# Two half-height products of a filter step, issued one right behind the other

## The chip, the cores and the metric

The kernel runs on one core of a Trainium2 chip. The metric is device time in microseconds (us) of one execution; less is better. Engines are named as in the profile: PE is TensorE (matrix products), PEld its weight loads, DVE is VectorE, ACT is ScalarE, POOL is GpSimd, SP is SyncE, which here only issues DMAs. Each engine works through its own list of instructions in order and waits at an instruction until what it needs is there.

## The reference

The reference is one layer of a hybrid encoder over a sequence of 2048 positions with 1024 channels: an input projection, a Hyena group (long convolutions with generated filters), an mLSTM group, an output projection, cross-attention and an MLP. The change touches only the generation of the Hyena filters, a small network over position features, whose last layer has 64 inputs:

```python
def _hyena_filter_spectrum(L, w1, b1, fr1, w2, b2, fr2, w3):
    ...
    hid = jnp.sin(fr1.astype(f32) * (z @ w1.astype(f32) + b1.astype(f32)))
    hid = jnp.sin(fr2.astype(f32) * (hid @ w2.astype(f32) + b2.astype(f32)))
    filt = (hid @ w3.astype(f32)).reshape(L, HYENA_ORDER, FILTER_DIRS, D_HYENA)
    ...
    filt = filt * jnp.exp(-t * jnp.abs(deltas))[:, None, None, :]
    fwd = filt[:, :, 0]
    bwd = jnp.flip(filt[1:, :, 1], axis=0)
    two_sided = jnp.concatenate([fwd, jnp.zeros((1, HYENA_ORDER, D_HYENA), f32), bwd], axis=0)
    return jnp.fft.rfft(two_sided, axis=0)
```

There are two orders and two directions, so 4 x 512 filter channels. Forward and backward filters are windowed, joined and transformed; the transforms are matrix products with constant matrices.

## The kernel before

The program is a string of stages. Two generators are woven into each other: `filters` with the first part of the input projection (`sweep`), then `hyena` with the rest of it; the mLSTM, the attention and the MLP follow. Weaving gives the order in which the instructions are written down. The order in which they stand on each engine is drawn from that by a scheduler, which works with a timeline of its own, so a changed dependency can move instructions far behind it.

The projection's products are the background work of PE. A product in high precision is split into three products of F32R halves (`mm3`, L336 to L338), each 128 x 128 by 512 columns, accumulated in a bank `mm`. Its results are copied by ACT (L685), convolved over three positions by ACT and DVE (L699 to L702), turned by PE (L719, 128-column products in which the identity is an operand), copied by ACT or DVE (L174, L176) and stored. New weights are split by ACT and DVE (L341, in `split`), new columns of `x` are scaled by DVE (L461) and split.

`filters` first computes the hidden layer `hid` (L239, L243, with the sine in between on DVE and ACT). `hid` holds two copies of the 64 hidden units: partitions 0 to 63 for forward positions, 64 to 127 for backward ones. The output layer then runs in 32 steps (16 blocks of positions by 2 orders). Each step:

- takes two banks `hy`, `pf` and `pb`;
- L286 multiplies `hid[0:64]` with `w3[0:64]` into `pf`, L287 multiplies `hid[64:128]` with `w3[64:128]` into `pb`. Both are plain fp32 products over 64 partitions, half of the array's height, and each leaves two records in the trace;
- DVE multiplies both with the decay windows (L289 reads `pf`, L290 reads `pb`), which ends the use of the banks;
- DVE adds the two (L294), POOL subtracts them (L295);
- `front` of the step before is issued (`late` holds it back by one step): two full-height fp32 products with `f1` (L271) into two more banks `hy`, ACT copies them out (L272), and SP stores them as `fs` every second step (L274).

There are four banks `hy`, taken in turn. A step takes four: two for L286 and L287, two for the L271 of the step before it. So the banks of a step's L286 and L287 are those that L286 and L287 of the previous step had, and they come free when DVE has run that step's L289 and L290. L286 waits for the first of them, L287 for the second, each by itself, and the scheduler may put other products between the two.

After the 32 steps the second transform follows (`blocks`): SP loads `fs` back (L305) and matrices (L301), PE multiplies (L319), ACT copies (L320), SP stores `hd` (L321). `hyena` reads `hd` later; its forward products are L856 and L880, its inverse ones L846 and L899.

Of the kernel before, what the change touches and what calls it, by code (L numbers as in the profile page):

```python
# [9 lines left out]
F32 = mybir.dt.float32  # L10
# [115 lines left out]
class Prog:  # L126
    def __init__(self, ctx, tc, a):
        self.tc, self.nc, self.a = tc, tc.nc, a
        nc = self.nc
        self.ctx = ctx  # L130
        self.dr = ctx.enter_context(tc.tile_pool(name="dr", bufs=1, space=DRAM))
        self.s = {}
        cp = self.cp = ctx.enter_context(tc.tile_pool(name="cp", bufs=1))
        ident = cp.tile([128, 128], F32, name="ident")
        nc.gpsimd.memset(ident, 1.0)
        nc.gpsimd.affine_select(ident, ident, pattern=[[-1, 128]], compare_op=ALU.is_equal, fill=0.0,
                                base=0, channel_multiplier=1)
        self.ident = ident
        self.eps = cp.tile([128, 1], F32, name="eps")
        nc.vector.memset(self.eps, EPS)  # L140
        self.ones = cp.tile([128, 128], F32, name="ones")
        nc.vector.memset(self.ones, 1.0)
        self.flip = 0
        self.pending = []
        self.prepq = None
        self.mid = None
        self.rbp = cp.tile([128, 16], F32, name="rbp")
        par = self.par = cp.tile([128, 192], F32, name="par")
        nc.scalar.dma_start(out=par, in_=a["par"])
        self.g_mix, self.g_mem, self.gx, self.gf = (par[:, 8 * i:8 * i + 8] for i in range(4))  # L150
        self.cw = par[:, 32:92].rearrange("p (i c) -> p i c", i=3)
        self.cb, self.gb = par[:, 92:112], par[:, 112:128]
        self.ps = ctx.enter_context(tc.tile_pool(name="ps", bufs=1, space=PSUM))
# [2 lines left out]
        return self.ps.tile([128, 512], F32, tag="mm", name="mm", bufs=4)  # L156

    def hy(self):
        return self.ps.tile([128, 512], F32, tag="hy", name="hy", bufs=4)

    def dram(self, name, shape):
        if name not in self.s:
# [42 lines left out]
    def filters(self):  # L205
        nc, tc, a = self.nc, self.tc, self.a
# [3 lines left out]
        if True:  # L210
            fw = sb.tile([128, 1280], F32, name="fw")
            nc.scalar.dma_start(out=fw, in_=a["fw"])
            w1, w2, w3 = fw[0:66, 0:128], fw[:, 128:256], fw[:, 256:1280].rearrange("p (o c) -> p o c", o=2)
# [18 lines left out]
            hid = sb.tile([128, 16, 128], F32, name="hid")  # L232
# [17 lines left out]
            def windows(j2):  # L250
                if j2 == 8:
                    return None
                w = ta(), ta()
                for r in range(2):
                    d = nc.sync.dma_start(out=w[r], in_=wv[r, :, 2 * j2:2 * j2 + 2])
                    if j2 < 2:
                        tc.keep_in_program_order(d)
                return w

            held = []  # L260

            def late(f):
                if held:
                    held.pop()()
                if f is not None:
                    held.append(f)

            def front(e, st, jj, o, js):
                for p in range(2):
                    pp = self.hy()  # L270
                    nc.tensor.matmul(pp, f1[:, p], e[p], start=True, stop=True)  # L271
                    nc.scalar.copy(st[p][:, jj], pp)  # L272
                    if jj == 1:
                        nc.sync.dma_start(out=sd[o][p, :, js], in_=st[p])  # L274

            nxt = windows(0)
            for j2 in range(8):
                js = slice(2 * j2, 2 * j2 + 2)
                yield 14
                (wf, wb), nxt = nxt, windows(j2 + 1)  # L280
                for o in range(2):
                    st = [ta() for p in range(2)]
                    for jj in range(2):
                        j = 2 * j2 + jj
                        pf, pb = self.hy(), self.hy()
                        nc.tensor.matmul(pf, hid[0:64, j], w3[0:64, o], start=True, stop=True)  # L286
                        nc.tensor.matmul(pb, hid[64:128, j], w3[64:128, o], start=True, stop=True)  # L287
                        f, b = tb(), tb()
                        nc.vector.tensor_tensor(f, pf, wf[:, jj], ALU.mult)  # L289
                        nc.vector.tensor_tensor(b, pb, wb[:, jj], ALU.mult)  # L290
                        if j == 0:
                            nc.vector.tensor_tensor(f[0:1], f[0:1], (skip, skip2)[o][0:1], ALU.add)
                        e = [tb() for p in range(2)]
                        nc.vector.tensor_tensor(e[0], f, b, ALU.add)  # L294
                        nc.gpsimd.tensor_tensor(e[1], f, b, ALU.subtract)  # L295
                        late(lambda e=e, st=st, jj=jj, o=o, js=js: front(e, st, jj, o, js))
# [13 lines left out]
            for n, (o, i) in enumerate(order):  # L310
                if True:
                    yield 3.4
                    dm, t = q.pop(0)
# [14 lines left out]
    def ta(self):  # L328
        return self.fsb.tile([128, 2, CH], F32, tag="a", name="a", bufs=7)

    def tb(self):
        return self.fsb.tile([128, CH], F32, tag="b", name="b", bufs=8)
# [1535 lines left out]
```

## Time and profile before

| | |
|---|---|
| median of 3 runs | 3330.34 us (3326.27 to 3330.63) |
| profiled execution | 3330.7 us |
| its span, first to last instruction | 3329.0 us |
| mean granted clock of PE | 0.980 |
| DMA | 655.70 MB, mean 197 GB/s |
| records of L286 and of L287 | 64 each, from 119.6 to 348.5 us |
| records of L271 | 128, from 127.6 to 357.0 us |
| records of L319 | 128, from 364.7 to 483.7 us |

A profile shows one execution. In a row of the timeline stand start, duration, engine, line, operation, tiles (out<-in), shape and count, then in brackets the idle time of the engine before it. A matrix product's duration is from its start until its last result, and products overlap in the array, so what a product costs PE is read from the distance of starts. "Waits" are times in which an engine stood idle before an instruction, by what released it. In tables by stretches each row is one window of the span.

### The profile page before, as it was taken

The numbers are of one execution on the slowest core, as the hardware profiler recorded it, in microseconds if no ns is written. First come the engines' busy times: TensorE is split into PE (matmuls) and PEld (weight loads), VectorE is DVE, ScalarE is ACT, GpSimd is POOL, SyncE is SP. The second block draws the span as 40 slices with busy tenths as digits, with TensorE's granted clock in tenths as the row PEclk, the third lists the DMA queues.
The fourth block names the chain that finished last, engine by engine and source line by source line (L and its number), as shares of the span: only waits on it lengthen the run. The fifth ranks groups of instructions, "written<-read, shape, count | busy, mean of one in ns | idle before, by whom it ended". The sixth has DMA issues, their size and how long they took to land.

```text
span 3329.0 us, 45394 instructions
## 1 busy us (share of the span) xinstructions
PE 3162.2 (95%) x15293; PEld 2519.0 (76%) x15293; DVE 1985.2 (60%) x3334; ACT 1512.1 (45%) x2860; POOL 1253.5 (38%) x863
## 2 busy tenths in 40 slices
PE   6999999899999988699999998999999999999998
PEld 5655666667667887598888896888788887888876
DVE  7684324534556656576766564755755576656595
ACT  5442444642564344354454444555655543333335
POOL 0132000220122204634434114876765564434483
PEclk9999999999999999799999999999999999999999
DMA  5554897886787659857557525764754475444434
GB/s 177 177 195 135 284 316 244 241 262 237 217 225 251 211 182 310 262 155 246 172 179 238 191 89 175 229 216 155 222 172 144 161 240 169 127 143 138 130 93 167
DMA packets 472257, 655.70 MB, mean 197 GB/s; under 512 B 39630, under 2 KB 251854, under 8 KB 471000
## 3 DMA queue, kind: packets, MB, share of 16 engines
q1 hardware_dynamic: 436404, 594.23, 56.4%
q10 hardware_dynamic: 35620, 58.57, 4.8%
q8 instruction: 121, 1.98, 0.3%
q14 instruction: 112, 0.92, 0.1%
HBM read 437.67 MB, written 214.99 MB: 196 GB/s over the span
## 4 chain that ended last, share of the span: by engine, by line
PE 49%; DMA 4%; DVE 3%; issue 2%; POOL 1%; ACT 1%; SPq 0%; DVEq 0%; POOLq 0%; ACTq 0%
PE mm L338 10%; PE mm L336 10%; PE mm L337 10%; PE hy L338 5%; PE hy L336 5%; PE hy L337 5%; DMA rw<-rows 1%; DVE wl L341 1%; PE hy L1135 1%; DMA wr<-xs 1%; PE hy L1137 1%; PE hy L1370 0%; PE hy L1266 0%; DMA wn<-in_w_out_dram 0%; DMA wr<-in_ff_w_dram 0%
## 5 line engine op out<-in xcount | busy, mean ns | idle before, releaser
L341 DVE TENSOR_TENSOR wl<-wn,wh 128x512 fp32r<-128x512 f32 (+1 forms) x364 | 293.5, 841 | 124.3 <-ACT wh L341 111.4
L1449 DVE TENSOR_TENSOR bl<-wr,bh 128x512 fp32r<-128x512 f32 x213 | 239.0, 1128 | 130.5 <-ACT bh L1448 126.8
L1448 ACT CAST ah<-w 128x512 fp32r<-128x512 f32 x284 | 176.2, 622 | 301.0 <-PE hy L337 152.2
L885 POOL TENSOR_TENSOR b<-b,a 128x512 f32<-128x512 f32 x64 | 89.4, 1397 | 586.7 <-ACT b L883 351.1
L341 ACT CAST wh<-wn 128x512 fp32r<-128x512 f32 (+1 forms) x364 | 208.9, 618 | 198.3 <-PE mm L337 54.9
L336 PE MATMUL mm<-xh,wh 128*128 128x512 f32 x640 | 279.4, 438 | 6.6 <-ACT xh L496 2.7
L337 PE MATMUL mm<-xl,wh 128*128 128x512 f32 x640 | 276.8, 433 | 0.1
L338 PE MATMUL mm<-xh,wl 128*128 128x512 f32 x640 | 265.8, 416 | 0.0
L1449 DVE TENSOR_TENSOR al<-w,ah 128x512 fp32r<-128x512 f32 x236 | 219.1, 930 | 58.6 <-ACT ah L1448 58.3
L1448 ACT CAST bh<-wr 128x512 fp32r<-128x512 f32 x232 | 143.6, 621 | 235.7 <-PE mm L338 171.3
L338 PE MATMUL mm<-bh,al 128*128 128x512 f32 x576 | 225.5, 394 | 7.4 <-DVE al L1449 4.5
L336 PE MATMUL mm<-bh,ah 128*128 128x512 f32 x576 | 226.8, 394 | 0.1
L337 PE MATMUL mm<-bl,ah 128*128 128x512 f32 x576 | 225.8, 392 | 0.0
L336 PE MATMUL mm<-act,wh 128*128 128x512 f32 x512 | 200.1, 395 | 1.0 <-ACT wh L341 1.0
L337 PE MATMUL mm<-act,wh 128*128 128x512 f32 x512 | 200.7, 392 | 0.0
L338 PE MATMUL mm<-act,wl 128*128 128x512 f32 x512 | 199.1, 392 | 0.0
L1305 POOL TENSOR_TENSOR ssum<-ssum,sq 128x512 f32<-128x512 f32 x56 | 79.0, 1411 | 277.4 <-ACT sq L1304 274.3
L336 PE MATMUL hy<-bh,ah 128*128 128x512 f32 x448 | 175.2, 391 | 0.0
L337 PE MATMUL hy<-bl,ah 128*128 128x512 f32 x448 | 174.6, 390 | 0.0
L338 PE MATMUL hy<-bh,al 128*128 128x512 f32 x448 | 174.4, 390 | 0.0
L295 POOL TENSOR_TENSOR b<-b 128x512 f32<-128x512 f32 x32 | 66.5, 2079 | 284.6 <-DVE b L290 147.8
L336 PEld LDWEIGHTS mm<-xh,wh 128*128 128x128 f32 x640 | 122.2, 191 | 63.9 <-issue 29.1
(360 smaller groups left out, 8922.9 us busy)
## 6 DMA issues: line engine op xcount, KB each, us to landing
wr<-hc SPq DMA_DIRECT2D x224, 256.0 KB
w<-in_ff_w_dram SPq DMA_DIRECT2D x176, 256.0 KB
hc<-t SPq DMA_DIRECT2D x128, 256.0 KB
wn<-in_w_in_dram SPq DMA_DIRECT2D x100, 256.0 KB
hc<-q SPq DMA_DIRECT2D x96, 256.0 KB
fs<-a SPq DMA_DIRECT2D x32, 512.0 KB
a<-fs SPq DMA_DIRECT2D x32, 512.0 KB
hd<-a SPq DMA_DIRECT2D x32, 512.0 KB
```

The source lines that it names most:

```text
L295: nc.gpsimd.tensor_tensor(e[1], f, b, ALU.subtract)
L336: mm(ps, lh, rh, start=start, stop=False)
L337: mm(ps, lh, rl, start=False, stop=False)
L338: mm(ps, ll, rh, start=False, stop=stop)
L341: both = (self.nc.scalar.copy(hi, src), self.nc.vector.tensor_tensor(lo, src, hi.bitcast(F32), ALU.subtract))
L885: nc.gpsimd.tensor_tensor(xt, xt, hi[:, m], ALU.mult)
L1135: nc.tensor.matmul(dst, nm[:, h], va[:, h], start=True, stop=state is None)
L1137: nc.tensor.matmul(dst, rows_[d, 1][:, h], state[:, h], start=False, stop=True)
L1305: nc.gpsimd.tensor_tensor(ssum, ssum, sq, ALU.add)
L1448: self.nc.scalar.copy(hi, src)
L1449: eng.tensor_tensor(lo, src, hi.bitcast(F32), ALU.subtract)
```

## The change

L286 and L287 are now issued by a helper, `beside`. It writes down the second product (into `pb`) first. It looks up, in a new list of the names of all `hy` banks taken so far, the two tiles that held the places of `pf` and `pb` four tiles before, finds the last instruction that read each of them, and makes the second product wait for both. The first product (into `pf`) is written down behind it, with a high priority, and pinned behind the last product written before it on PE, that is behind the second product. The products, their operands, the banks and all other instructions are as they were, and each engine has as many instructions as before.

```diff
     def hy(self):
-        return self.ps.tile([128, 512], F32, tag="hy", name="hy", bufs=4)
+        t = self.ps.tile([128, 512], F32, tag="hy", name="hy", bufs=4)
+        self.banks.append(t[:, 0:1].tensor.name)
+        return t
+
+    def beside(self, first, second):
+        n = self.banks.index(first[0].tensor.name)
+        n = self.banks.index(first[0].tensor.name)
+        held = self.banks[max(0, n - 4):max(0, n - 2)]
+        b = self.nc.tensor.matmul(*second, start=True, stop=True)
+        for i in reversed(self.nc.cur_bb.bb.instructions[-4000:]):
+            own = [x.bass_ap.tensor.name for x in i.ins if getattr(x, "bass_ap", None) is not None]
+            for t in [t for t in held if t in own]:
+                held.remove(t)
+                self.tc.add_manual_dep(b.ins, i.name, mybir.DependencyInfo(
+                    mybir.DependencyClass.Sync, mybir.DependencyReason.DATA), reason="beside")
+        with self.tc.high_priority(2000):
+            self.tc.keep_in_program_order(self.nc.tensor.matmul(*first, start=True, stop=True))
...
                         pf, pb = self.hy(), self.hy()
-                        nc.tensor.matmul(pf, hid[0:64, j], w3[0:64, o], start=True, stop=True)
-                        nc.tensor.matmul(pb, hid[64:128, j], w3[64:128, o], start=True, stop=True)
+                        self.beside((pf, hid[0:64, j], w3[0:64, o]), (pb, hid[64:128, j], w3[64:128, o]))
                         f, b = tb(), tb()
```

In the changed file the second product stands at L168, the first at L176, and all lines behind them are 16 to 17 later.

More of the change, by code (lines that the diff above doesn't have):

```diff
@@ L143, in __init__ @@
         self.flip = 0
+        self.banks = []
         self.pending = []
```

## The prediction

> **What bounds the kernel now.** I read the page first, for the share of each engine.
>
> ```profile
> span 3329.0 us, 45394 instructions
> PE 3162.2 (95%) x15293; PEld 2519.0 (76%) x15293; DVE 1985.2 (60%) x3334; ACT 1512.1 (45%) x2860; POOL 1253.5 (38%) x863
> ```
>
> PE is busy for 95% of the span and no other engine passes 60%. That is an average, so the table by stretches comes next. The columns are: stretch, its length, then busy time and count on PE, PEld, DVE, ACT, POOL, then granted clock, DMA share, GB/s. The first row is the stage of the change, the second its most crowded part, then the filters' second transform, the Hyena convolutions, the mLSTM's start.
>
> ```profile
> 119.00:350.00 231.00, 231.00 (x795) 129.82 (x794) 142.63 (x228) 83.08 (x133) 64.32 (x31) 1.00 0.46 153
> 160.00:205.00 45.00, 45.00 (x165) 27.11 (x165) 38.96 (x82) 19.81 (x30) 16.84 (x6) 1.00 0.53 178
> 350.00:500.00 150.00, 148.94 (x584) 100.70 (x583) 36.06 (x54) 67.10 (x114) 2.22 (x1) 1.00 0.94 323
> 500.00:1166.00 666.00, 637.28 (x3056) 469.88 (x3055) 358.42 (x595) 324.98 (x525) 124.33 (x86) 0.99 0.75 236
> 1166.00:1500.00 334.00, 277.23 (x1830) 254.25 (x1830) 201.77 (x533) 140.91 (x369) 124.50 (x98) 0.92 0.74 228
> ```
>
> In the stage of the change PE is busy 231.00 of 231.00 us at full clock: nothing but PE's own work sets its length. The waits of the stage, over all engines, say the same from the other side.
>
> ```profile
> POOL b L295 <- DVE b L290: 141.2, 28, 8.7
> ACT a L272 <- PE hy L271: 95.5, 45, 6.2
> DVE b L289 <- PE hy L286: 47.1, 17, 4.9
> DVE b L290 <- PE hy L287: 16.7, 18, 2.0
> ```
>
> DVE stands still 47.1 us for L286 and 16.7 us for L287, and ACT 95.5 us for L271: the readers of the banks wait for the products, not the products for the readers.
>
> **The change part by part.** *Pairing.* First the number of steps that it reaches. The records of L286 (count, shortest, median and longest in ns, first and last start), then the same table for L286 alone, for L287 alone, and for every product of `hid`, that is for both together:
>
> ```profile
> L286 PE MATMUL hy<-fw,hid x64: 589/589/693, 119.6 to 346.4; 64*128 64x512 f32 x64
> ...
> 119.00:350.00 231.00, 35.65 (x64) 9.50 (x64) 1.00 0.46 153
> 119.00:350.00 231.00, 35.65 (x64) 9.50 (x64) 1.00 0.46 153
> 119.00:350.00 231.00, 61.52 (x128) 16.33 (x128) 0.00 (x0) 1.00 0.46 153
> ```
>
> Each product leaves two records, so 64 are 32 steps, at 35.65 / 32 = 1.11 us. Together they cover 61.52 us, not 71.30: 9.78 us lie on top of each other, 9.78 / 1.11 = 9 steps. Those 9 are the ones in which nothing stands between the two products; in the other 23 something does. In the built order of the changed program all 32 stand with nothing between. Here is one step of each kind on PE (start, duration, line, tile, count), the split one first.
>
> ```profile
> 252.12 0.39 PE L336 MATMUL mm<-xh,wh 128*128 128x512 f32 x1
> 252.34 0.39 PE L337 MATMUL mm<-xl,wh 128*128 128x512 f32 x1
> 252.66 1.12 PE L286 MATMUL hy<-fw,hid 64*128 64x512 f32 x2
> 253.71 0.50 PE L338 MATMUL mm<-xh,wl 128*128 128x512 f32 x1
> 254.14 1.12 PE L287 MATMUL hy<-fw,hid 64*128 64x512 f32 x2
> 255.20 1.12 PE L271 MATMUL hy<-b,f 128*128 128x512 f32 x2
> ...
> 289.30 0.39 PE L338 MATMUL mm<-xh,wl 128*128 128x512 f32 x1
> 289.53 0.39 PE L336 MATMUL mm<-xh,wh 128*128 128x512 f32 x1
> 289.85 0.69 PE L286 MATMUL hy<-fw,hid 64*128 64x512 f32 x1
> 289.85 0.69 PE L287 MATMUL hy<-fw,hid 64*128 64x512 f32 x1
> 290.38 0.59 PE L286 MATMUL hy<-fw,hid 64*128 64x512 f32 x1
> 290.39 0.59 PE L287 MATMUL hy<-fw,hid 64*128 64x512 f32 x1
> 290.91 0.50 PE L337 MATMUL mm<-xl,wh 128*128 128x512 f32 x1
> 291.24 0.39 PE L338 MATMUL mm<-xh,wl 128*128 128x512 f32 x1
> ```
>
> Read starts, since durations overlap. An ordinary product of the projection holds PE 0.23 us (289.30 to 289.53). The one before a half-height product takes 0.32 (252.34 to 252.66) and the one behind it 0.33 (290.91 to 291.24): going into and out of the half-height form costs 0.09 and 0.10. The split step, from 252.34 to 255.20, is 2.86 us; less two ordinary slots (0.46), plus the way out that the L271 behind it hides (0.10), it is 2.50 us. The paired step, from 289.53 to 291.24, is 1.71 less 0.46, so 1.25 us: both products run in the time of one. A step that becomes a pair frees 2.50 - 1.25 = 1.25 us, and 23 of them free 28.7 us, all on the engine that sets the stage's length. No instruction is added or removed on any engine, and the 32 steps keep their own DMAs.
>
> *The hold.* Now L287 goes first and waits until DVE has read both banks of the step before, by L289 and by L290; L286 follows. Before, L286 waited for L289 alone. Behind the waiting product stands the projection on PE, and for that wait ACT (L685 and the splits), then DVE and the stores. The readers' rows (mean ns after the busy time), then a typical and the tightest step on DVE, and the first and last split step of that part on PE:
>
> ```profile
> L289 DVE TENSOR_TENSOR b<-hy,a 128x512 f32<-128x512 f32 x32 | 22.0, 688 | 50.3 <-PE hy L286 47.1 <-issue 2.0 <-PE hy L287 1.1
> L290 DVE TENSOR_TENSOR b<-hy,a 128x512 f32<-128x512 f32 x32 | 21.9, 686 | 16.7 <-PE hy L287 16.7
> L295 POOL TENSOR_TENSOR b<-b 128x512 f32<-128x512 f32 x31 | 64.3, 2075 | 277.9 <-DVE b L290 141.2 <-DVE P L680 122.5 <-PE hy L271 7.9
> ```
>
> ```profile
> 247.63 0.69 DVE L290 TENSOR_TENSOR b<-hy,a 128x512 f32<-128x512 f32 x1 [0.60 <-PE hy L287]
> 253.89 0.69 DVE L289 TENSOR_TENSOR b<-hy,a 128x512 f32<-128x512 f32 x1 [4.24 <-PE hy L286]
> ...
> 188.10 0.68 DVE L290 TENSOR_TENSOR b<-hy,a 128x512 f32<-128x512 f32 x1
> ```
>
> ```profile
> 164.71 1.12 PE L286 MATMUL hy<-fw,hid 64*128 64x512 f32 x2
> ...
> 189.74 1.12 PE L286 MATMUL hy<-fw,hid 64*128 64x512 f32 x2
> ```
>
> Typically L290 ends at 248.32 and the next step's first product starts at 252.66: 4.3 us to spare. In the crowded part it ends at 188.78 against 189.74: 0.96 us to spare. There DVE does 38.96 us of work in 45, since the next columns of `x` are prepared then. Three of the steps between 160 and 205 are split, the first at 164.71, the last at 189.74; pairing brings PE 3 x 1.25 = 3.8 us forward there, 2.8 us beyond the spare. Bounds: no gain below nothing, as PE has no idle time to lose, and at most one L290 in each of 31 steps, 31 x 0.69 = 21.3 us. I take 3 us, by the tightest row. The other consumers have room: a step lasts (346.4 - 119.6) / 31 = 7.3 us by the first and last start of L286, of which POOL's L295 needs 2.08, and from the start of L286 to the end of L295 pass 1.23 (252.66 to 253.89) + 0.69 + 0.69 + 2.08, about 4.7 us, while the L271 that needs it stands behind the next pair.
>
> A rule that speaks against pairing stands in the Trainium skill, TensorEngine Tiling (Array Packing), section PSUM Bottleneck: products that run side by side speed up TensorE but not the reading of the banks, which may become the limit. Here the two reads take 0.69 + 0.69 = 1.38 us against 1.06 for the pair, so by that rule the pair would be paced by DVE; the trace disagrees on average, since those 1.38 us come once in 7.3, and comes near to it from 160 to 205 alone.
>
> *The order behind it.* The scheduler draws the order anew up to the middle of the program. The products of the second transform (L319) stand on average 39 places later against the projection, the Hyena's inverse products (L846) 19 later at first and not at all from their middle on; in the mLSTM some products change places. At 0.23 us, 39 places are 9 us of projection that used to lie behind the filters, as cover for the Hyena's chain, and now lies before it. What such cover is worth, the longest waits of PE from 350 to 1166 show:
>
> ```profile
> PE hy L846 <- DVE b L886: 7.4, 7, 1.6
> PE mm L336 <- ACT st L174: 6.2, 3, 4.0
> PE mm L743 <- DVE st L176: 5.0, 1, 5.0
> ```
>
> PE idles 666 - 637.28 = 28.7 us from 500 to 1166, in pieces of a microsecond to five. Bounds: 9 us lost if all of the cover is missed; 11 us won if the waits of 6.2 and 5.0 are dissolved by chance. I take 4 lost, since the chain already waits there. For the mLSTM (334 - 277.23 = 56.8 us idle) I take nothing, with 8 to either side by the size of a few such waits. From 350 to 500 DMA is at 0.94, but PE is busy 148.94 of 150: that stretch moves forward as a whole.
>
> *The sum.* The profiled execution took 3330.7 us (span 3329.0): 3330.7 - 28.7 + 3 + 4 = 3309.0. The median of the runs, 3330.34, is 0.4 below the profiled one, so 3308.6; I say 3309.
>
> **The rivals.**
> 1. *The Hyena gives most of it back.* The convolutions' chain, not PE, sets when the stage ends, and PE waits longer in it. For: 28.7 us of idle PE already, and 9 us less cover. Against: PE is busy 637.28 of 666. With 9 us of cover, 8 in the mLSTM and 3 for the hold gone, 28.7 - 20 = 9 are left: 3322.
> 2. *The pair does not overlap in the new order.* All 9 pairs in the trace have L286 ahead; now L287 is. Were they to run one after the other, 23 steps would save one way in and out (0.2 us each, 4.6) and 9 would lose 1.05 each (252.66 to 253.71; 9.5): 3335. Against: 0.01 us between the starts (290.38, 290.39) shows no preference for a side.
> 3. *Slower: the hold becomes a stall at the head of PE's queue.* L290 stands on DVE behind work of the projection (L341, L176) whose products lie behind the held L287; the two queues then take turns instead of overlapping. A turn costs the way from product to reader, 1.23, plus 0.69 for L290, 1.9 us. It decides from 28.7 / 31 = 0.93 us a step on; with 20 of 31 steps caught it is 38 us, so 3340. For: DVE is busy 142.63 of 202 us once the stage is shorter, 71%, and 38.96 of 41 in the crowd. Against: 4.3 us to spare in the typical step, and DVE's 63.8 us of waiting for just these products.
> 4. *DVE's reads set the pace* wherever it is crowded: none of the 3.8 us from 160 to 205 is kept. That is 1 us beyond my 3, and gives 3310; it lies inside the forecast.
>
> **How the numbers follow.** Forecast with rival 4: 65%, its own range 3296 (28.7 and half of the 11 won) to 3317 (hold 3, cover 9, and 3 of the mLSTM lost). Rival 1, from 3317 to 3327: 14%. Rival 2, 3327 to 3337: 7%. Rival 3: 9%. More than 34 us won: 5%. The range 3295 to 3327 leaves out some 2 in 10. About 0.2%, 6.7 us, is what a measurement here can tell from no change, so faster means below 3323.7: the forecast, the larger gain and two thirds of rival 1, 0.79. Slower means above 3337: rival 3 and the edge of 2, 0.10. The rest, 0.11, is the same.
>
> **What would show each step.** Pairing: all 32 steps with L286 and L287 starting within 0.01 us, and the products of `hid` covering about 36 us in place of 61.52. Its worth: the time from the first start of L286 to the last down from 227 us to between 198 and 204. The hold: waits of PE at L287's new line for DVE, 3 us in total and in the crowded part alone; above 29 us it is rival 3. The order: PE's idle time in the Hyena's 666 us at 28.7 before, about 33 after; if it is over 45, rival 1. I am wrong at the root if the stage shortens by less than 15 us although all pairs overlap, for then something other than PE held it.

## The result and the profile after

The changed kernel takes 3301.7 us (median of 4 runs, 3294.94 to 3305.1) against 3330.49 before: ratio 0.9911, 95% interval 0.9896 to 0.9925, so 25 to 35 us less. Measured again later (e11 below), the ratio was 0.9921, 0.9904 to 0.9937. The profiled execution took 3300.1 us. Its page begins:

```profile
span 3298.4 us, 45399 instructions
PE 3131.6 (95%) x15293; PEld 2510.5 (76%) x15293; DVE 1989.7 (60%) x3334; ACT 1513.6 (46%) x2860; POOL 1246.8 (38%) x863
```

PE has 30.6 us less to do and the span is 30.6 us shorter, with the same 15293 records. The row of the products of `hid`, from the table by stretches, and a step on PE (in the new file L168 is the product into `pb`, L176 the one into `pf`, L288 what was L271):

```profile
119.00:340.00 221.00, 36.45 (x128) 9.72 (x128) 0.00 (x0) 0.99 0.51 168
```

```profile
251.74 0.62 PE L735 MATMUL mm<-ident,cv 128*65 128x128 f32 x4
252.29 0.69 PE L168 MATMUL hy<-fw,hid 64*128 64x512 f32 x1
252.30 0.69 PE L176 MATMUL hy<-fw,hid 64*128 64x512 f32 x1
252.83 0.59 PE L168 MATMUL hy<-fw,hid 64*128 64x512 f32 x1
252.84 0.59 PE L176 MATMUL hy<-fw,hid 64*128 64x512 f32 x1
253.35 1.13 PE L288 MATMUL hy<-b,f 128*128 128x512 f32 x2
```

All 32 steps look like this one: the two products start within 0.01 us of each other, and together they cover 36.45 us in place of 61.52.

To see where the time came from, stretches of equal work have to be compared. The new order moves some projection products into the filters' stage, so equal names are not equal work; I divided both traces at the same counts of PE records instead (the x after PE's busy time). Columns as in the prediction. First before, then after: the filters' output layer, the first part of the Hyena, its second part, the start of the mLSTM, the rest.

```profile
119.00:360.00 241.00, 241.00 (x840) 136.98 (x839) 147.11 (x234) 87.08 (x140) 66.54 (x32) 1.00 0.48 159
...
465.00:674.00 209.00, 198.99 (x802) 138.77 (x801) 96.56 (x149) 111.67 (x173) 28.27 (x20) 0.98 0.78 246
674.00:1167.00 493.00, 474.05 (x2402) 356.60 (x2401) 272.15 (x462) 227.07 (x376) 96.06 (x66) 0.99 0.74 234
1167.00:1498.00 331.00, 274.23 (x1805) 251.25 (x1804) 199.55 (x528) 139.88 (x366) 124.50 (x98) 0.92 0.74 228
1498.00:3329.00 1831.00, 1779.95 (x8691) 1498.99 (x8689) 1162.95 (x1748) 830.18 (x1590) 937.39 (x641) 0.99 0.54 173
```

```profile
119.00:338.00 219.00, 214.18 (x843) 131.99 (x841) 148.45 (x235) 86.23 (x137) 61.68 (x32) 0.99 0.51 167
...
443.00:646.00 203.00, 199.17 (x802) 137.20 (x800) 95.39 (x144) 113.08 (x174) 25.72 (x19) 0.99 0.85 268
646.00:1142.00 496.00, 476.17 (x2402) 358.44 (x2401) 276.83 (x465) 230.16 (x381) 99.07 (x69) 0.98 0.75 234
1142.00:1470.00 328.00, 271.02 (x1806) 247.86 (x1805) 196.02 (x526) 140.21 (x366) 123.03 (x97) 0.92 0.74 228
1470.00:3298.00 1828.00, 1777.79 (x8693) 1497.78 (x8691) 1165.77 (x1750) 830.19 (x1590) 935.67 (x641) 0.99 0.54 173
```

The filters' stretch gives 22 us, the Hyena's first part 6; the second part loses 3, and the mLSTM and the rest give 3 each. In the filters' stretch PE's busy time fell by 26.8 us, but PE, which never idled there before, now idles 4.8 us (219.00 - 214.18). PE's waits in that stretch say why:

```profile
PE mm L352 <- ACT xh L357: 2.5, 1, 2.5
PE mm L469 <- DVE dg L463: 0.7, 1, 0.7
PE hy L288 <- DVE xr_y L219: 0.6, 1, 0.6
PE hy L168 <- DVE b L306: 0.4, 2, 0.2
PE mm L353 <- DVE xl L357: 0.4, 1, 0.4
PE hy L288 <- POOL b L311: 0.2, 1, 0.2
```

The held product L168 waited 0.4 us in all. Most of the rest is for the preparation of `x`, which comes late around 180 us. The longest wait, of 2.5 us, ends with the cast of `xh` on ACT. Here are that cast and the one before it on ACT, then the scaling on DVE whose result it reads:

```profile
180.30 0.62 ACT L357 CAST wh<-wn 128x512 fp32r<-128x512 f32 x1 [4.83 <-DMA wn<-in_w_in_dram]
180.83 1.04 ACT L357 CAST xh<-xt 128x1024 fp32r<-128x1024 f32 x1
...
177.41 1.40 DVE L477 SCALAR_TENSOR_TENSOR xt<-xt,par,rb 128x512 f32<-128x512 f32 x2
```

DVE was done with `xt` at 178.81, but the cast began only at 180.83: before it on ACT stands the cast of new weights, and for their transfer ACT had been idle for 4.83 us. So some 2.0 of these 2.5 us, an estimate from the three rows, come by way of a late transfer. SP issued it at 175.49, and had waited before that for DVE to free buffers (4.8, 3.2 and 0.8 us from 163 on); as far as these waits show, DVE's crowd of work stands at the start of this chain. After the longest wait the granted clock falls to half for a while (row of the stretch just behind it; the clock stands ahead of the DMA share):

```profile
183.20:186.20 3.00, 2.64 (x8) 1.48 (x5) 3.00 (x5) 1.06 (x2) 3.00 (x1) 0.51 1.01 361
```

The whole stretch has 0.99, so 1% of 219 us or some 2 us more went there. DVE waits for the products less than before, yet still does (rows of all engines' waits; before, 47.1 us for the first product and 16.7 for the second):

```profile
DVE b L305 <- PE hy L176: 33.6, 18, 4.3
ACT P L701 <- PE mm L354: 22.5, 13, 4.8
```

In the Hyena's first part PE's waits were, before and after:

```profile
PE mm L336 <- ACT st L174: 4.0, 1, 4.0
PE hy L846 <- DVE b L886: 2.6, 3, 1.3
PE hy L846 <- ACT cv L704: 2.4, 1, 2.4
```

```profile
PE hy L862 <- DVE b L902: 3.2, 3, 1.9
```

Two waits of 4.0 and 2.4 us have gone: the redrawn order won there, where the prediction had it lose.

### The profile page after: what moved, and what is told of

Same layout as the page of the kernel before. It is cut to its first block, busy times and chain, and to the rows that moved or that the text cites. A ratio compares the mean times of both kernels' runs of the same rounds, so it can differ in the third digit from the quotient of the medians.

```text
span 3298.4 us, 45399 instructions
## 1 busy us (share of the span) xinstructions
PE 3131.6 (95%) x15293; PEld 2510.5 (76%) x15293; DVE 1989.7 (60%) x3334; ACT 1513.6 (46%) x2860; POOL 1246.8 (38%) x863
## 4 chain that ended last, share of the span: by engine, by line
PE 75%; DMA 10%; DVE 5%; issue 4%; ACT 3%; POOL 2%; SPq 1%; ACTq 0%; DVEq 0%; POOLq 0%
PE mm L352 15%; PE mm L354 15%; PE mm L353 15%; PE hy L352 5%; PE hy L354 5%; PE hy L353 5%; DMA a<-hd 2%; PE hy L872 2%; PE hy L335 2%; PE hy L288 2%; PE hy L915 1%; DVE wl L357 1%; DMA rw<-rows 1%; PE mm L735 1%; PE hy L168 1%
## 5 line engine op out<-in xcount | busy, mean ns | idle before, releaser
L357 DVE TENSOR_TENSOR wl<-wn,wh 128x512 fp32r<-128x512 f32 (+1 forms) x364 | 286.3, 821 | 122.4 <-ACT wh L357 120.9
L1465 DVE TENSOR_TENSOR al<-w,ah 128x512 fp32r<-128x512 f32 x236 | 226.3, 960 | 60.8 <-ACT ah L1464 60.3
```

The source lines that it names most:

```text
L357: both = (self.nc.scalar.copy(hi, src), self.nc.vector.tensor_tensor(lo, src, hi.bitcast(F32), ALU.subtract))
L1465: eng.tensor_tensor(lo, src, hi.bitcast(F32), ALU.subtract)
```

## The experiments

Ratios are to the kernel before on the same chip, with 95% intervals; "windows" are stretches of equal PE records as above.

**e1: the pairs adjacent, but not side by side.** The order of instructions on every engine is that of the changed kernel, one for one.

```diff
-self.beside((pf, hid[0:64, j], w3[0:64, o]), (pb, hid[64:128, j], w3[64:128, o]))
+self.beside((pf, hid[0:64, j], w3[0:64, o]), (pb, hid[0:64, j], w3[0:64, o]))
```

> The second product reads the forward half of the hidden layer and of the weights (partitions 0 to 63), as the first does; so the backward filters are those of the forward half. PE's order is that of the changed kernel, instruction for instruction, and all 32 steps stand with nothing between. If the gain is the two products running side by side, they now run one after the other: two more records of 0.43 us (120.15 to 120.58 in the trace of before) in each of 32 steps, 27.5 us, so about 3329 us. If the gain comes from the order that the scheduler drew anew, the time stays near 3302. If the new order is worth the 8 us by which the result beat the sum, and the pairing the rest, it comes between: before's 23 split steps cost 2.50 and its 9 pairs 1.25, 68.8 us together, the 32 here 2.11 each, 67.5, so 3329 less 8, about 3321.

Measured: 3330.7 us, 0.9991 (0.9980 to 1.0003). A step on PE, then the filters' stretch and the Hyena's first part of e1:

```profile
256.20 0.39 PE L353 MATMUL mm<-xl,wh 128*128 128x512 f32 x1
256.51 1.12 PE L168 MATMUL hy<-fw,hid 64*128 64x512 f32 x2
257.48 1.02 PE L176 MATMUL hy<-fw,hid 64*128 64x512 f32 x2
258.43 0.50 PE L354 MATMUL mm<-xh,wl 128*128 128x512 f32 x1
258.76 0.59 PE L288 MATMUL hy<-b,f 128*128 128x512 f32 x1
```

```profile
116.00:360.00 244.00, 241.77 (x840) 144.46 (x839) 147.55 (x235) 86.54 (x137) 59.53 (x32) 0.99 0.46 151
...
466.00:668.00 202.00, 198.79 (x801) 137.14 (x800) 95.23 (x146) 113.60 (x175) 25.99 (x19) 0.99 0.85 271
```

The step takes 258.76 - 256.20 less two ordinary slots, 2.10 us, as expected, against 1.25 in a pair: 0.85 x 32 = 27.2 us. The stretch is 244 us against 219, and the whole gain is gone. That does not make standing next to each other worthless. By the prices of a step, the 32 steps of e1 cost 67.2 us (32 x 2.10) and those of the kernel before 68.8 (23 x 2.50 and 9 x 1.25). Adjacency saves 0.40 us in each of 23 split steps, 9.2 us, and e1 loses again the overlap of the 9 steps that had it before, 7.7 us. So of the 28.7 us of the prediction 9.2 are adjacency, and 19.6 are running side by side. What parts e1 from the changed kernel is the overlap in all 32 steps: 0.0080 of the time, 27 us, against the result, and 23 and 19 us against e11 and e4, which have the same order. The Hyena's first part is as short as in the changed kernel, 202 against 209 before, without any pairing: that share of the gain does belong to the order. In the whole time of e1 it does not show beyond its interval.

**e2 and e3: fewer pairs.** e2 uses the helper in half of the steps; e3 leaves the wait out.

```diff
+                        if o == 0:
                             self.beside((pf, hid[0:64, j], w3[0:64, o]), (pb, hid[64:128, j], w3[64:128, o]))
+                        else:
+                            nc.tensor.matmul(pf, hid[0:64, j], w3[0:64, o], start=True, stop=True)
+                            nc.tensor.matmul(pb, hid[64:128, j], w3[64:128, o], start=True, stop=True)
```

> The helper is used for the first order's steps alone, the second order's are issued as before. In the built order 23 steps stand with nothing between, 14 more than before. Pairing at 1.25 us a step gives 14 x 1.25 = 17.5 us: 3313 us. A gain that comes from the order drawn anew has no reason to follow the count of pairs.

```diff
         b = self.nc.tensor.matmul(*second, start=True, stop=True)
-        for i in reversed(self.nc.cur_bb.bb.instructions[-4000:]):
...
-                    mybir.DependencyClass.Sync, mybir.DependencyReason.DATA), reason="beside")
         with self.tc.high_priority(2000):
```

> The wait for both banks is left out, the pin and the priority stay. In the built order 25 steps stand with nothing between, 16 more than before: 16 x 1.25 = 20 us, 3310.5 us. If the wait is what costs (the 3 us of the prediction), PE idles less than 4.8 us in the filters' output layer; if the crowd of DVE work costs it, PE idles there as in the changed kernel.

Measured: e2 3322.1 us, 0.9976 (0.9965 to 0.9987), with 23 pairs; e3 3319.6 us, 0.9964 (0.9953 to 0.9974), with 24 pairs in the trace, not 25. Both gained 8 to 9 us less than I expected. The filters' stretch alone shows how much of it is pairing:

| kernel | pairs | stretch, us | idle PE in it, us |
|---|---|---|---|
| e8 (below) | 5 | 253 | 4.4 |
| before | 9 | 241 | 0.0 |
| e2 | 23 | 230 | 5.1 |
| e3 | 24 | 228 | 3.2 |
| changed, e4, e11 | 32 | 219 | 4.8, 4.1, 4.8 |

Without the idle time the stretches fall from 241 (9) over 224.9 (23) and 224.8 (24) to 214.2 (32): 23 more pairs save 26.8 us, 1.17 a pair, near the 1.25 of the sum. (e8, 248.6 without its idle time, lies some 3 us above that line, at a granted clock of 0.99 in place of 1.00.) e2 and e3 also lack the shorter part of the Hyena (209 and 208 us), since its order there is that of before. And e3 idles 3.2 us, all between 182 and 193, without any hold, so most of the idle time is not the hold's.

**e4: the wait without the pin and the priority.**

```diff
-        with self.tc.high_priority(2000):
-            self.tc.keep_in_program_order(self.nc.tensor.matmul(*first, start=True, stop=True))
+        self.nc.tensor.matmul(*first, start=True, stop=True)
```

> The pin and the priority are left out, the wait for both banks stays. PE's built order is that of e3, instruction for instruction, with 25 steps paired, so the two differ by the wait alone. If the wait costs nothing, the ratio to before is that of e3, 0.9964, within its interval. If it stalls PE, it is slower than e3, by 31 x 0.69 = 21 us at most.

Measured: 3308.7 us, 0.9933 (0.9915 to 0.9951). The expectation names the wrong neighbour: the order is that of the changed kernel on every engine, with 32 pairs, so this is the changed kernel again. The wait does the work: once the second product is held until both banks are free, nothing is left that would part the two. The pin alone leaves 8 steps split. It also shows what scatters: its stretches are 219, 203, 494 and 336 us, the changed kernel's 219, 203, 496 and 328. The same instructions take 8 us more in the start of the mLSTM.

**e6: two steps at a time.** Four half-height products together, so half as many ways in and out of that form.

```diff
+        held = self.banks[max(0, n - 4):n]
+        own = slice(0, 64), slice(64, 128)
+        todo = [(banks[q][h], hid[own[h], j + q], w3[own[h], o]) for q in range(2) for h in (1, 0)]
+        b = self.nc.tensor.matmul(*todo[0], start=True, stop=True)
...
+            for t in todo[1:]:
+                self.tc.keep_in_program_order(self.nc.tensor.matmul(*t, start=True, stop=True))
```

> Both steps of an order's pair of positions are issued together: four half-height products with nothing between, held until all four banks are free, and the full-height products of the group before are issued ahead of them. Going into and out of the half-height form then happens 16 times in place of 32, at 0.39 us (1.25 less two records of 0.43): 6.2 us less, 3295 to 3296. The rival: all four banks have to be read before the next group, and the filters' steps stand later against the projection (their last product 183 places later in PE's order), so PE waits in the filters or the Hyena behind them misses its cover, and the time is above 3302.

Measured: 3299.8 us, 0.9907 (0.9894 to 0.9920). On PE, a group, then PE's longest waits in the filters of e6 (L192 is the line of the last three products, L304 what was L271):

```profile
153.93 0.39 PE L376 MATMUL mm<-xh,wl 128*128 128x512 f32 x1
154.25 0.69 PE L183 MATMUL hy<-fw,hid 64*128 64x512 f32 x1
...
156.17 0.50 PE L374 MATMUL mm<-xh,wh 128*128 128x512 f32 x1
156.51 0.40 PE L375 MATMUL mm<-xl,wh 128*128 128x512 f32 x1
```

```profile
PE hy L304 <- DVE b L331: 4.9, 3, 2.6
PE mm L375 <- DVE xl L379: 3.6, 1, 3.6
```

The group takes 156.51 - 153.93 - 0.46 = 2.12 us, 0.38 less than two pairs: the size was right, 16 x 0.38 = 6.1 us. PE waits longer in the filters, as the rival said, 8.5 us in the two rows, but not so long that the time rises above 3302. From the start of the stage to the start of the mLSTM e6 needs 1016 us for 4440 PE records, the changed kernel 1023 for 4442. Over the whole time 1.9 us are left, less than the intervals can tell.

**e5, e7, e8: DVE relieved.** The low halves of the prepared `x` go to POOL, in the changed kernel, in e6 and in the kernel before.

```diff
     def scaled(self, x, k0, gain, rb, hi, lo):
         for k in range(x.shape[1]):
             self.gained(x[:, k], gain[:, k0 + k:k0 + k + 1], rb)
-        self.split(hi, lo, x)
+        self.nc.scalar.copy(hi, x)
+        self.nc.gpsimd.tensor_tensor(lo, x, hi.bitcast(F32), ALU.subtract)
```

> The changed kernel with the low halves of the prepared x (8 subtractions of 128x1024 in the filters' stage, 1.245 us each on DVE) moved from DVE to POOL. If DVE's crowd is what costs the changed kernel its 4.8 us of idle PE in that stage, and with it 1.7 us of half clock, DVE has 10 us less to do there, PE's idle time in the stage falls to about 1 us, and the time to about 3296. If the held product itself is the cause, the idle time stays. The rival: POOL takes 2.08 us for 512 columns, so 4.2 for 1024, 33 us for the 8, its own L295 stands behind them, the products that read it (L271) come late, and nothing is won or some is lost.

> e6 with the same move. e6 idled 6.1 us in the stage; if that is DVE's crowd too, 5 us less than e6, 3295. Where the groups of four wait for their banks, the move does not help and the time is that of e6.

> The kernel before with the same move. PE never waited in its stage, so the relief of DVE wins nothing. In the built order 6 steps are paired in place of 9, which costs 3 x 1.25 = 3.8 us: 3334.

Measured: e5 3285.0 us, 0.9870 (0.9849 to 0.9891); e7 3311.3 us, 0.9950 (0.9934 to 0.9967); e8 3329.0 us, 0.9997 (0.9986 to 1.0009). e5 is faster than both kernels, but not for the reason I gave. Its filters' stretch, the Hyena's second part and the mLSTM's start, then PE's longest waits in the filters:

```profile
118.00:340.00 222.00, 214.07 (x841) 132.99 (x840) 146.60 (x223) 85.38 (x136) 77.81 (x39) 0.98 0.50 164
...
647.00:1128.00 481.00, 471.72 (x2403) 353.58 (x2402) 270.06 (x460) 231.38 (x382) 126.94 (x83) 1.00 0.76 244
1128.00:1457.00 329.00, 270.17 (x1803) 248.75 (x1802) 190.52 (x519) 135.15 (x364) 118.98 (x92) 0.90 0.74 227
```

```profile
PE mm L352 <- ACT xh L482: 4.2, 1, 4.2
PE mm L353 <- POOL xl L483: 3.2, 1, 3.2
```

In the filters PE idles 7.9 us, more than without the move. POOL hands one low half over late, 3.2 us; the rival was right that nothing is won there, but it had looked for the wait at the full-height products. The longer wait, 4.2 us, is again for the cast of `xh` on ACT, and again ACT stood idle for weights before it, 6.0 us here. Nor is DVE relieved in that stretch: the 9.7 us of low halves are gone from it, but its busy time falls only from 148.45 to 146.60, because other work takes longer there, the sums (L310 in both files) 953 ns on average in place of 779. So e5 does not test what a freer DVE would do for the filters. The gain lies in the Hyena's second part, 481 us against 496, where the second pass over `x` is prepared. The profiled execution is the slowest of e5's four, 3293.0 us against a median of 3285.0, so 8 us of its gain are in no trace. e8 shows the same in the kernel before (480 against 493), and there the filters lose it again: 253 us against 241, 5 pairs against 9 and 4.4 us idle. e7 is 11.5 us above e6, which neither case of its expectation gave: the move and the groups of four do not add up.

**e9, e10, e11: the move only behind the filters.**

```diff
+        if late:
+            self.nc.scalar.copy(hi, x)
+            self.nc.gpsimd.tensor_tensor(lo, x, hi.bitcast(F32), ALU.subtract)
+        else:
+            self.split(hi, lo, x)
...
-            self.scaled(xs.pop(0), 2 * j, self.g_mix, rb, *(t[(slice(None),) + to] for t in (self.xh, self.xl)))
+            self.scaled(xs.pop(0), 2 * j, self.g_mix, rb, *(t[(slice(None),) + to] for t in (self.xh, self.xl)), late=c < 2)
```

> The changed kernel with the move of e5 kept to the preparations after the filters (the second pass over x and mem); in the filters' stage the low halves stay on DVE, and PE's order is that of the changed kernel up to the Hyena. e5 and e8 both gained 12 to 15 us in the second half of the Hyena's stretch (idle PE 20 before, 9 with the move) and lost some in the filters' stage (7.9 of idle PE against 4.8, and 3.4 more of half clock). If that reading holds, this kernel keeps the gain without the loss: about 15 us below the changed kernel on this chip, 3286 to 3288, and PE idle 4.8 in the filters' stage. If e5's gain was the luck of one order, this one, drawn anew from the Hyena on, shows none of it: 3302.

> The kernel before with the same late move. If relieving DVE in the second half of the Hyena is worth 12 to 15 us whatever the filters do, the time is 3316 to 3318, and the pairing on top of it (e9) is worth what it was, 27 to 29 us. If the two gains are not independent, the distance to e9 is another.

> The changed kernel again, beside e9 and e10 on the same chip: 0.9911 of before. e4, whose instructions stand in the same order on every engine, gave 0.9933, so the two should meet within their intervals.

Measured: e9 3301.8 us, 0.9904 (0.9886 to 0.9922); e10 3315.7 us, 0.9949 (0.9932 to 0.9966); e11 3305.0 us, 0.9921. e10's time came as expected. e9's did not: 3302 is what its expectation gave for the case that e5's gain was the luck of one order. So the pairing on top of the late move is worth 14 us (3315.7 to 3301.8), half of the 27 to 29 expected of it. Filters, Hyena's second part and mLSTM's start of e9, then the latter two of e11, then the last of e10:

```profile
120.00:339.00 219.00, 214.97 (x841) 132.69 (x840) 148.09 (x234) 85.81 (x137) 62.00 (x32) 0.98 0.51 168
...
647.00:1125.00 478.00, 470.45 (x2399) 354.02 (x2398) 267.54 (x454) 229.08 (x378) 126.32 (x79) 1.00 0.77 242
1125.00:1466.00 341.00, 274.78 (x1806) 255.18 (x1806) 192.94 (x527) 138.67 (x366) 120.03 (x96) 0.89 0.73 221
```

```profile
648.00:1141.00 493.00, 475.14 (x2399) 356.98 (x2398) 275.57 (x465) 229.32 (x380) 97.78 (x67) 0.99 0.74 235
1141.00:1472.00 331.00, 269.84 (x1801) 247.37 (x1800) 193.28 (x526) 140.24 (x366) 124.11 (x98) 0.91 0.73 228
```

```profile
1153.00:1476.00 323.00, 267.13 (x1807) 245.94 (x1806) 192.93 (x521) 134.87 (x364) 118.52 (x92) 0.91 0.76 232
```

The 15 us are there when the Hyena ends (478 against 493), and 10 of them are gone when the mLSTM has started (341 against 331): PE idles 66 us there, against 61, and the clock falls to 0.89. Against e10 it loses 18 us there (341 against 323), of 23 won in the filters (219 against 242) and 8 in the Hyena (203 and 478 against 209 and 480). The gain in the Hyena's second part is not the luck of one order: it takes 478 to 481 us in e5, e8, e9 and e10, which have three different orders there. (In e6 and e7 that stretch holds other work and can't be compared.) In the mLSTM's start, PE's order is one and the same in e5, e8 and e10, which take 329, 325 and 323 us, and another in e9. But e9's 341 is one trace, and the changed kernel and e4 differ by 8 us there in one and the same order. What costs e9 these 10 us, and whether e5 would keep its lead under another order, stays open.

## Why the prediction was right

*Pairing.* The count was right: 23 split steps became pairs, and the products of `hid` cover 36.45 us where "about 36" was expected. The size was right as well: 28.7 us forecast, 26.8 less busy time of PE in the stage, with some 2 us of half clock in it. By e1, two thirds of that come from running side by side; the rest is one way into the half-height form and out of it less in each of the 23 steps.

*The hold.* The sum had 3 us, where the run shows some 6.5: 4.8 idle and about 2 of half clock. The place was right, the crowded part near 180 us, but the mechanism was not the hold, so that the term was of the right order is luck. L168 waited 0.4 us, and e3 idles there without the wait. PE, 1.25 us faster in each newly paired step, comes to the products of the next `x` before it is prepared, and the longest wait comes by way of weights that arrive late on ACT, behind waits of SP for DVE. e5 was to test DVE's part and does not, since DVE was busy there for 2 us less only; so what would take this wait away stays open.

*The order behind it.* This is the term that failed: +4 was taken for the Hyena, between 9 lost and 11 won, and it won. Its first part is 6 us shorter, and it is shorter in every kernel with this order: 203 (changed), 203 (e4), 205 (e11), 202 (e1, without pairs), against 209 before, 209 (e2) and 208 (e3), in which PE's order there is that of before. The upper bound, waits of PE dissolved by chance, was the better picture, though only one of those it named went, the 4.0 us of L336; the 5.0 us of L743 is still there with 4.5 (L759 now), and 2.4 us went that it had not named. The loss of cover did not come about: in the Hyena's two parts PE idles 23.7 us against 29.0 before, where about 33 were expected. What the profiled execution won behind it, 3 and 3 less 3, is scatter: the same instructions took 328, 331, 334 and 336 us in the mLSTM's start.

*The sum.* With what was measured, 26.8 less busy time, 4.8 more idle time in the filters and 6 won in the Hyena's first part, -26.8 + 4.8 - 6 = -28.0, and the medians differ by 28.8. The forecast of 3309 was 7 us too high. That is what two errors of opposite sign leave: the order was 10 us too dear, the hold's term some 3.5 too cheap.

*What would show each step.* The test by first and last start of L286 was badly made. I expected 198 to 204 us; it is 335.1 - 120.6 = 214.5. The new order puts 44 more products between the two, some 10 us, and I had that order before me. By the same slip the stage "shortens by less than 15 us although all pairs overlap", by 12, which was the sign of being wrong at the root; at equal work it shortens by 22.

*The rivals.* The Hyena gave nothing back (1). The pair overlaps with the second product ahead just as well, 0.01 us apart in all 32 steps (2); e1, in which two products do run one after the other in every step, takes 3330.7 us and not the 3335 of that rival, since a way in and out costs 0.39 us and not 0.2. The hold never became a stall (3). DVE's reads (4) set no pace on average: DVE still waited 33.6 us for the first product. The rule of the Trainium skill (TensorEngine Tiling (Array Packing), PSUM Bottleneck) that the reading of the banks may become the limit is thus not borne out by this trace for the two reads themselves.

## What to carry to other kernels

Two products over half of the array's height are worth placing back to back when PE is the bound: here a pair costs 1.25 us, two apart 2.50, two adjacent in the same rows 2.10, so adjacency alone brings a third of the gain. Here the scheduler parted them where their buffers came free one by one; one wait for both was enough to keep them together, and cost 0.4 us of waiting, because the readers were early. Where a scheduler draws the order anew, compare stretches of equal work: of 15 us gained in one stage (e9), 10 were gone in the next, for a reason that stays open.

## What the runs showed of the hardware

Going into the half-height form and out again costs more than the neighbours show. In e1 two products in the same rows take 2.10 us, four records of 0.43 us and 0.39 us beside; the same 0.38 was saved once for every two steps in e6. The prediction saw 0.19 of it, in the products before and behind, and had the rest inside its 1.05 us; the sum was not touched. One rule fits all four forms: 0.39 us for each way in and out, and 0.43 for each pass, where a pair's two products share their passes. Two products apart make 2 x 0.39 + 4 x 0.43 = 2.50, two in the same rows 0.39 + 4 x 0.43 = 2.11 (2.10 measured), a pair 0.39 + 2 x 0.43 = 1.25, a group of four 0.39 + 4 x 0.43 = 2.11 (2.12 measured). The Trainium skill says in TensorEngine Tiling (Array Packing), Key Properties, that changing the tiling mode drains TensorE; the trace agrees as far as it shows a price, 0.39 us for both changes, and none between two half-height products.
